# An encoder layer on one core: the FFN norm factor carried to the last norm, a running PSUM bank in the FFN input, and all pair weights of the FFN output prepared there

## The chip, the core and the metric

The kernel runs on one core of a Trainium2 chip. The core has five engines with queues of their own: TensorE (PE; its weight loads are listed apart as PEld), VectorE (DVE), ScalarE (ACT), GpSimd (POOL) and SyncE (SP). Each runs its own instructions in order and waits on semaphores for the others. All DMAs of this kernel are issued from SP's queue, in order. The metric is the device time of one launch in microseconds (us), the median of several launches.

## The reference

An encoder layer is applied to two sequences of 512 tokens (1024 tokens together, model width 1024), each with a memory of 256 rows: a norm, three branches (a state-space scan, a differential attention, a cross-attention on the memory), gates, an output projection, and then the part that the change touches:

```python
    x = x + merged @ p['w_out'][l]
    xn2 = _rmsnorm(x, p['norm_ffn'][l])
    gate, up = jnp.split(xn2 @ p['w_ffn_in'][l], 2, axis=-1)
    return x + (jax.nn.silu(gate) * up) @ p['w_ffn_out'][l]
    ...
    return _rmsnorm(x, p['norm_final'])
```

with `_rmsnorm(x, g) = x * rsqrt(mean(x*x) + 1e-6) * g`, and an FFN width of 2816.

## The kernel before

All is float32. Each product is made of three TensorE matmuls on rounded halves (`split`, L131: a ScalarE copy to the high half, a VectorE subtraction for the low half): high x high, high x low, low x high. Activations lie with features on the partitions, 128 at a time, and the 1024 tokens on the free side, the two sequences as two halves of 512 (`L`). The matmuls around the change have 512 columns.

**Seven products instead of eight.** The FFN's two matrix products take 2 x 2 blocks (two feature blocks, two halves of the tokens) and form them with seven products of sums and differences. The weights' names are A11, A12, A22 (plain blocks) and S1 to S4 (sums, made by POOL); the operands' sums stand in `ops` and `pairs`. The results are four quadrants: in the FFN input c11 and c12 are the gate of the two sequences, c21 and c22 the up part; in the FFN output they are two output tiles of 128 features by two sequences.

**FFN input** (L1134, 22 tiles, i = 0 to 21). A tile multiplies two 128-column weight blocks, one of w_fg and one of w_fu. `weights4` (L1002) loads both (`wf`, two buffers, L1006 and L1007), splits A11, A12 and A22, lets POOL form S1 to S4 (L1022 to L1025), and splits these. `products` (L1071) runs the seven products in the order A11, S2, A12, S3, S1, A22, S4, each into its own PSUM bank, 12 matmuls each. `quadrants` (L1104) copies the first bank by ScalarE (L1107) and forms the quadrants by six VectorE sums (`summed`, L1098, L1101), each of a bank and an SBUF tile. Then, per sequence: VectorE multiplies the gate by the norm's factor (`accs`, L1163), ScalarE takes a tanh (L1164), POOL multiplies up by the factor (L1165), VectorE multiplies twice (L1166, L1167) into `ac`, which goes to DRAM as aD. In tile 0 the factor is made out of the sums of squares: ones matmuls, a square root, a reciprocal, transposes and a copy (`rstd`, `factor`, L187 to L202).

**FFN output** (L1246). 12 visits cover four pairs of output tiles; within a visit a few pairs of FFN blocks are accumulated into seven banks (`VISITS`, 36 pieces in all, 21 matmuls each), then `quadrants` forms four results, which POOL adds to `y`. y was loaded from x1D, the residual that the output projection stored (L961). The weights of a piece are seven split blocks, `weights7` (L1213), loaded two pieces ahead.

**Pieces prepared early.** `prepare` (L459) is a generator that works on pieces ahead of time: load the raw blocks (two DMAs, L442), split three of them (`part(n_, 4, ...)`), form four sums on POOL (`raw_sums`, L451), split these (`part(n_, 0, ...)`), and store the halves to DRAM (`wD`). `half_piece` (L491) runs one step of it. `NPREP = (16, 28)`: pieces 0 to 15 are prepared with all seven blocks within the cross-attention's steps (L728), pieces 16 to 27 with the four sums alone within FFN input tiles 1 to 18 (L1170). For pieces 16 to 27 the three plain blocks, and for 28 to 35 all seven, are made on the spot in the FFN output.

**The end.** After the pairs come the last four FFN blocks as plain products, tile by tile of y, with sums of squares; `final` (L1313) makes the last norm's factor and stores the output.

**What sets the order.** A scheduler places the instructions of each engine by priorities and a model of their times, except where they are kept in written order (`PE.on`, L57) or held behind another instruction (`tc.issue_after`). TensorE is in written order through the attention stages and from the last FFN input tile on; in FFN input tiles 0 to 20 it was the scheduler's. Buffers of a pool are handed round; an instruction that writes one waits for the last reader of what was there.

Of the kernel before, what the change touches and what calls it, by code (L numbers as in the profile page):

```python
# [39 lines left out]
NPREP = (16, 28)  # L40
# [32 lines left out]
def encoder(ctx: ExitStack, tc: tile.TileContext, a, out):  # L73
# [109 lines left out]

    def new_acc():
        return rp.tile([P, L], F32, tag="acc", name="acc", bufs=2)
# [9 lines left out]
    def factor(ss, n, nt=4, bias=epsc):  # L195

        rs = rp.tile([P, 4], F32, tag="rs", name="rs", bufs=4)
        S.activation(out=rs[:, :nt], in_=ss[:, :nt], func=AF.Sqrt, scale=1.0 / n, bias=bias)
        V.reciprocal(rs[:, :nt], rs[:, :nt])
        bc = aux()  # L200
        for t in range(nt):
            PE.transpose(bc[:, t * P : (t + 1) * P], rs[:, t : t + 1].broadcast_to([P, P]), ident)  # L202
        return rs, bc
# [235 lines left out]
    pieces = [(m, p, 7 if i < NPREP[0] else 4 if i < NPREP[1] else 0) for i, (m, p) in enumerate(pieces)]  # L439
# [19 lines left out]
    def prepare(es_, todo_):  # L459
# [130 lines left out]
    prep = prepare(pes, pieces[: NPREP[0]])  # L590
    next(prep)


# [97 lines left out]
    for i in range(-AHEAD, len(steps) + 1):  # L691
# [36 lines left out]
        half_piece(last_e)  # L728
    while queue:
        fill(6)  # L730
    assert next(prep, None) is None
    pes.close()
# [327 lines left out]
    def product(ps, w, o, ks=range(4)):  # L1060
        wh, wl = w
        for k in ks:
            th, tl = ops[k]
            ws_ = slice(k * P, (k + 1) * P)
            PE.matmul(ps, wh[:, ws_], th[:, o], start=(k == 0), stop=False)
            PE.matmul(ps, wh[:, ws_], tl[:, o], start=False, stop=False)
            PE.matmul(ps, wl[:, ws_], th[:, o], start=False, stop=(k == 3))
# [48 lines left out]

    def act_pair(p, tag="ts", third=PO):
# [16 lines left out]
    for i in range(KFF):  # L1134
        w = nxt_w or all7(i)
        nxt_w = None
        if i == 1:
            prep = prepare(pes, pieces[NPREP[0] : NPREP[1]])
# [10 lines left out]
        ps = products(i, w)  # L1149
        p0 = next(ps)  # L1150
        if i == 0:
            for s in range(NS):
                _, bc = rstd(accs[s], DM)
                S.copy(accs[s], bc)
        gf0, gf1, up0, up1 = quadrants(ps, p0)
        ac = ap2.tile([P, NT], F32, tag="ac", name="ac")
        with ExitStack() as es_:
# [3 lines left out]
            for s, gf, up in ((0, gf0, up0), (1, gf1, up1)):  # L1161
# [3 lines left out]
                PO.tensor_tensor(out=up, in0=up, in1=accs[s], op=ALU.mult)  # L1165
                V.scalar_tensor_tensor(out=ac[:, cs], in0=ac[:, cs], scalar=1.0, in1=gf, op0=ALU.add, op1=ALU.mult)  # L1166
# [132 lines left out]
    def ones(ss, sq, n, start=False, stop=False):  # L1299

        for t in range(n // P):
            PE.matmul(ss[:, t : t + 1], sq[:, t * P : (t + 1) * P], onec[:, 0:1], start=(start and t == 0),
                      stop=(stop and t == n // P - 1))

    def column_sums(acc, n):
        ss = aux()
        ones(ss, acc, n, True, True)
# [25 lines left out]
    for c, n in ((0, L), (L, L // 2), (L + L // 2, L // 2)):  # L1333
        acc = new_acc()
        for m in range(KD):
            if c == 0:
                if m == 0:
                    kept.insert(0, weight(last_rows(m), nb * P))
                if m < KD - 1:
                    with yielding(last_s if m == 0 else last_7):  # L1340
# [14 lines left out]
            if m == KD - 3:  # L1355
                ss = aux()
                ones(ss, acc, n, start=True)
# [8 lines left out]
        end = final(ss if c + n == NT else column_sums(acc, n), c, n, ready, (2, 3) if c == L else ())  # L1366
# [425 lines left out]
```

## Time and profile before

| | us |
|---|---|
| median of 3 launches | 1603.34 (1603.12 to 1603.37) |
| span of the profiled launch | 1603.0 |
| cross-attention with the early pieces | about 386 to 530 |
| FFN input, tiles 1 to 20, one unbroken run of matmuls | 971.7 to 1351.7 |
| FFN output, pieces | about 1352 to 1545 |
| last four blocks, last norm | 1545 to 1603 |

The profile is one launch, taken by the hardware profiler. In a row, "x" and a number is a count; "ns" or a plain number after busy time is the mean of one; a duration of a matmul covers its whole way through the array, so that rows overlap, and the pace is read from start to start or from a count per stretch. "<-" names what ended an idle time. Lines (L...) are those of the kernel before. In the table of stretches each engine has its busy time and, after x, its instructions; then follow the clock granted to TensorE, the share of the DMA engines' time, and GB/s. In the list of waits the numbers are the sum in us, the count and the longest.

### The profile page before, as it was taken

How to read it: one execution, taken by the hardware profiler on the slowest of the kernel's cores; microseconds unless marked ns; L12 is line 12 of the kernel's file. 1: busy time of each engine (PE TensorE's matmuls, PEld its weight loads, DVE VectorE, ACT ScalarE, POOL GpSimd, SP SyncE). 2: the span in 40 equal slices, each digit the busy share in tenths (PEclk: the TensorE clock that was granted, in tenths of full speed). 3: DMA queues.
4: the chain of work that ended last, by engine and by line, in shares of the span. 5: the costliest groups of instructions: out<-in, count | busy, mean ns of one | idle time of the engine just before them, and what ended most of it. 6: DMA issues, size and time to landing. Idle time of an engine off the chain costs nothing.

```text
span 1603.0 us, 21625 instructions
## 1 busy us (share of the span) xinstructions
PE 1587.1 (99%) x7838; PEld 1314.8 (82%) x7838; DVE 1162.9 (73%) x1856; ACT 640.0 (40%) x1142; POOL 541.6 (34%) x449
## 2 busy tenths in 40 slices
PE   9999999999999999999999999999999999999997
PEld 7888788888898778778878878888888888788877
DVE  7976996076773766776465678888898778988654
ACT  6544323274652455574133443332333323233323
POOL 0010100001333220300343367676665553444653
PEclk9999999999999999999999999999999999999998
DMA  9554523576762111244454432333323223986222
GB/s 366 173 160 150 179 95 125 180 273 201 252 224 102 54 47 40 73 156 140 145 190 132 144 118 80 131 119 129 121 106 118 79 88 119 344 332 198 80 66 106
DMA packets 104891, 237.86 MB, mean 148 GB/s; under 512 B 13520, under 2 KB 45008, under 8 KB 104784
## 3 DMA queue, kind: packets, MB, share of 16 engines
q1 hardware_dynamic: 104784, 236.47, 43.1%
q8 instruction: 62, 1.02, 0.3%
q14 instruction: 45, 0.37, 0.1%
HBM read 165.16 MB, written 71.27 MB: 147 GB/s over the span
## 4 chain that ended last, share of the span: by engine, by line
PE 87%; issue 4%; DVE 3%; DMA 3%; POOL 2%; ACT 0%; SPq 0%; POOLq 0%; DVEq 0%; ACTq 0%
PE bkmm L66 75%; PE bksc L66 3%; PE bktr L66 2%; PE bkoo L66 2%; PE bktr L69 2%; DVE tl L135 1%; PE bktr L1626 1%; POOL mg L793 1%; PE bktr L1597 1%; DMA yt<-bD 1%; PE bktr L1686 0%; PE bktr L1687 0%; PE bktr L1685 0%; PE bktr L1565 0%; DMA acc<-in_w_fo 0%
## 5 line engine op out<-in xcount | busy, mean ns | idle before, releaser
L66 PE MATMUL bkmm<-xh,wh 128*128 128x512 f32 x640 | 255.4, 399 | 0.0
L66 PE MATMUL bkmm<-xh,wl 128*128 128x512 f32 x640 | 250.9, 392 | 0.0
L66 PE MATMUL bkmm<-xl,wh 128*128 128x512 f32 x640 | 250.5, 391 | 0.0
L66 PE MATMUL bkmm<-tl,wh 128*128 128x512 f32 (+1 forms) x621 | 241.2, 388 | 1.4 <-DVE tl L135 1.4
L66 PE MATMUL bkmm<-th,wl 128*128 128x512 f32 (+1 forms) x621 | 241.0, 389 | 0.9 <-DVE wl L135 0.9
L66 PE MATMUL bkmm<-th,wh 128*128 128x512 f32 (+1 forms) x621 | 241.1, 389 | 0.0
L134 ACT CAST wh<-wf 128x1024 fp32r<-128x1024 f32 (+1 forms) x134 | 117.9, 880 | 224.1 <-PE bkmm L66 179.8
L135 DVE TENSOR_TENSOR wl<-wf,wh 128x1024 fp32r<-128x1024 f32 (+1 forms) x134 | 145.1, 1083 | 50.2 <-ACT wh L134 45.7
L66 PEld LDWEIGHTS bkmm<-xh,wh 128*128 128x128 f32 x640 | 120.3, 188 | 30.3 <-issue 7.9
L66 PE MATMUL bkmm<-th,w 128*128 128x512 f32 x432 | 141.5, 392 | 2.7 <-DVE up L1101 1.0
L66 PEld LDWEIGHTS bkmm<-xh,wl 128*128 128x128 f32 x640 | 120.2, 188 | 26.7 <-issue 1.3
L66 PEld LDWEIGHTS bkmm<-xl,wh 128*128 128x128 f32 x640 | 120.4, 188 | 22.4 <-issue 0.4
L66 PEld LDWEIGHTS bkmm<-tl,wh 128*128 128x128 f32 x621 | 116.6, 188 | 25.9 <-DVE tl L135 2.1
L66 PEld LDWEIGHTS bkmm<-th,wl 128*128 128x128 f32 x621 | 116.5, 188 | 25.7 <-DVE wl L135 1.7
L66 PEld LDWEIGHTS bkmm<-th,wh 128*128 128x128 f32 x621 | 116.6, 188 | 23.9
L1165 POOL TENSOR_TENSOR up<-up,acc 128x512 f32<-128x512 f32 x44 | 83.6, 1920 | 87.8 <-DVE up L1101 87.8
L454 POOL TENSOR_TENSOR raw<-raw 128x128 f32<-128x128 f32 x28 | 15.2, 545 | 284.4 <-DVE nb L545 206.5
L66 PEld LDWEIGHTS bkmm<-th,w 128*128 128x128 f32 x432 | 80.9, 188 | 23.8 <-DVE up L1101 3.4
L793 POOL TENSOR_TENSOR mg<-mg,gl 128x1024 f32<-128x1024 f32 x16 | 43.5, 2720 | 139.0 <-DVE gl L789 139.0
L548 ACT ACTIVATE e<-bksc,nb 128x512 f32<-128x512 f32 (+1 forms) x96 | 58.8, 615 | 73.5 <-DVE nb L543 51.9
L66 PE MATMUL bkmm<-tl,w 128*128 128x512 f32 x216 | 84.2, 390 | 0.0
L66 PE MATMUL bkmm<-yh,wh 128*128 128x512 f32 x192 | 75.9, 397 | 0.8 <-ACT wh L134 0.4
(641 smaller groups left out, 3527.8 us busy)
## 6 DMA issues: line engine op xcount, KB each, us to landing
wf<-in_w_in SPq DMA_DIRECT2D x40, 512.0 KB, 3.9
wD<-hl SPq DMA_DIRECT2D x28, 512.0 KB, 2.9
w<-wD SPq DMA_DIRECT2D x28, 512.0 KB, 5.0
gD<-gt SPq DMA_DIRECT2D x24, 512.0 KB, 2.8
gl<-gD SPq DMA_DIRECT2D x24, 512.0 KB, 3.4
wf<-in_w_fg SPq DMA_DIRECT2D x22, 512.0 KB, 3.7
wf<-in_w_fu SPq DMA_DIRECT2D x22, 512.0 KB, 3.6
aD<-ac SPq DMA_DIRECT2D x22, 512.0 KB, 3.1
```

The lines of the kernel that those rows point to most:

```text
L66: return self.put(self.eng.matmul(*args, **kw))
L69: return self.put(self.eng.transpose(*args, **kw))
L134: h = S.copy(hi, src)
L135: l_ = V.tensor_tensor(out=lo, in0=src, in1=hi.bitcast(F32), op=ALU.subtract)
L454: PO.tensor_tensor(out=a22, in0=a21, in1=a22, op=ALU.add)
L548: last_x = S.activation(out=e, in_=sc, func=AF.Exp, bias=nb, scale=scale, accum_out=sm)
L793: PO.tensor_tensor(out=mg[m], in0=mg[m], in1=gt, op=ALU.add)
L1165: PO.tensor_tensor(out=up, in0=up, in1=accs[s], op=ALU.mult)
L1597: PE.matmul(kp[64 * hf : 64 * hf + 48, g * 144 : (g + 1) * 144], l_[:, 2 * hf + g, :], o_[:, 4 * g4 + 2 * hf + g, :], start=(l_ is lr48), ...
L1626: PE.matmul(ps[:, g * P : (g + 1) * P], w_[:, gg * P : (gg + 1) * P], u_[:, 8 * o + gg, :], start=True, stop=True)
```

## The change

Four things are changed.

1. **The factor is carried through.** The FFN's up part is no longer multiplied by the norm's factor, so the FFN's result is too large by 1/factor = `root` per token. The residual is multiplied by root too: eight times, x1D is loaded, multiplied by POOL with root (broadcast over the partitions: `rbc`, four transposes and a copy per sequence), and stored again. The last norm then works on root times the true sum; its epsilon is replaced by `eroot` = eps x 1024 x root^2 per token, which a small matmul puts ahead of the sums of squares (`least`), and its square root takes a bias of 0 (`zeroc`).
2. **A running bank.** In tiles 1 to 20 `running` takes the place of `products` and `quadrants`. A11, S2, S3 and A22 are accumulated, one after the other, into the same bank `pu`; ScalarE copies pu after A11, S2 and S3, and VectorE forms c11, u4, c22 and c12 with these copies: four sums. The fourth quadrant is pu itself, read by the last multiplication. The products run in the order A11, A12, S2, S1, S3, S4, A22.
3. **All 36 pieces are prepared beside it**, all with seven blocks, none in the cross-attention: `between` runs a step at three places of a tile and the old place runs a fourth, so two pieces per tile for tiles 1 to 18. The buffers of the split halves are one of each size (there were two of the larger). The FFN output only loads.
4. **Order and room.** TensorE is in written order from tile 1. `mbc`, used much earlier, moves to another pool.

```diff
-NPREP = (16, 28)
+NPREP = 36
...
-    pieces = [(m, p, 7 if i < NPREP[0] else 4 if i < NPREP[1] else 0) for i, (m, p) in enumerate(pieces)]
+    pieces = [(m, p, 7 if i < NPREP else 0) for i, (m, p) in enumerate(pieces)]
...
-            hl = pq.tile([P, k, 2, P], F32R, tag=f"hl{k}", name="hl", bufs=k // 2)
+            hl = pq.tile([P, k, 2, P], F32R, tag=f"hl{k}", name="hl", bufs=1)
...
-        mbc = cst.tile([P, L], F32, name="mbc")
+        mbc = new_acc()
...
-    prep = prepare(pes, pieces[: NPREP[0]])
-    next(prep)
...
-        half_piece(last_e)
...
+    def running(w, between):
+
+        def copied(tag):
+            t_ = ap2.tile([P, L], F32, tag=tag, name=tag)
+            S.copy(t_, pu)
+            return t_
+
+        of = dict(SEVEN)
+        pu, pv = bank(), bank()
+        product(pu, w["A11"], of["A11"])
+        product(pv, w["A12"], of["A12"])
+        c11 = summed("gf", pv, copied("p1"), 2)
+        between()
+        product(pu, w["S2"], of["S2"], more=True)
+        pw = bank()
+        product(pw, w["S1"], of["S1"])
+        u4 = summed("p1", pw, copied("u2"))
+        between()
+        product(pu, w["S3"], of["S3"], more=True)
+        px = bank()
+        product(px, w["S4"], of["S4"])
+        c22 = summed("up", pw, copied("u3"), 2)
+        c12 = summed("gf", px, u4, 2)
+        between()
+        product(pu, w["A22"], of["A22"], more=True)
+        return c11, c12, pu, c22
...
+        def between():
+            if 1 <= i < KFF - 3:
+                half_piece((last_sum,))
+
+        PE.on = i > 0
+        if i in (0, KFF - 1):
+            ps = products(i, w)
+            p0 = next(ps)
+            if i == 0:
+                for s in range(NS):
+                    rt = root[:, 4 * s : 4 * s + 4]
...
+                    S.activation(out=rt, in_=ss[:, :4], func=AF.Sqrt, scale=1.0 / DM, bias=epsc)
+                    rs = rp.tile([P, 4], F32, tag="rs", name="rs", bufs=4)
+                    V.reciprocal(rs, rt)
+                    S.copy(accs[s], spread(rs))
+                    V.scalar_tensor_tensor(out=eroot[:, 4 * s : 4 * s + 4], in0=rt, scalar=EPS * DM, in1=rt, op0=ALU.mult, op1=ALU.mult)
...
+                for s in range(NS):
+                    S.copy(rbc[:, s * L : (s + 1) * L], spread(root[:, 4 * s : 4 * s + 4]))
+            gf0, gf1, up0, up1 = quadrants(ps, p0)
+        else:
+            gf0, gf1, up0, up1 = running(w, between)
...
-                PO.tensor_tensor(out=up, in0=up, in1=accs[s], op=ALU.mult)
...
+        if 2 <= i < 2 + KD:
+            xs_ = rbp.tile([P, NT], F32, tag="xs", name="xs")
+            nc.sync.dma_start(xs_, x1D[i - 2])
+            PO.tensor_tensor(out=xs_, in0=xs_, in1=rbc, op=ALU.mult)
+            nc.sync.dma_start(x1D[i - 2], xs_)
...
+    def least(c, n):
         ss = aux()
-        ones(ss, acc, n, True, True)
+        PE.matmul(ss[:, : n // P], ident, eroot[:, c // P : (c + n) // P], start=True, stop=False)
+        return ss
...
-        _, bc = factor(ss, DM, n // P)
+        _, bc = factor(ss, DM, n // P, zeroc)
```

More of the change, by code (lines that the diff above doesn't have):

```diff
@@ L1058, in encoder, with product @@
     aD = [drp.tile([P, NT], F32, name=f"aD{i}") for i in range(KFF)]
-    def product(ps, w, o, ks=range(4)):
+    def product(ps, w, o, ks=range(4), more=False):
         wh, wl = w
+        mark = {"skip_group_check": True} if more else {}
         for k in ks:
@@ L1147, in encoder @@
             PE.on = True
[L1149 to L1155, printed above, removed]
+        def between():
[8 more added lines that the diff above has]
+                    rt = root[:, 4 * s : 4 * s + 4]
+                    ss = aux()
+                    for t in range(4):
+                        PE.matmul(ss[:, t : t + 1], accs[s][:, t * P : (t + 1) * P], onec[:, 0:1], start=(t == 0), stop=(t == 3))
+                    S.activation(out=rt, in_=ss[:, :4], func=AF.Sqrt, scale=1.0 / DM, bias=epsc)
[3 more added lines that the diff above has]
+                    V.scalar_tensor_tensor(out=eroot[:, 4 * s : 4 * s + 4], in0=rt, scalar=EPS * DM, in1=rt, op0=ALU.mult, op1=ALU.mult)
+                rbp = pes.enter_context(tc.tile_pool(name="rb", bufs=1, side="right", reuse_waits="tile"))
+                rbc = rbp.tile([P, NT], F32, tag="rbc", name="rbc")
+                for s in range(NS):
[3 more added lines that the diff above has]
+            gf0, gf1, up0, up1 = running(w, between)
         ac = ap2.tile([P, NT], F32, tag="ac", name="ac")
```

35 lines of the change are left out of this document (20 added, 15 removed).

## The prediction

> **What bounds the kernel now.** I read the page first, then the stretches of the span, then the chain of waits and TensorE's waits by stretch.
>
> ```profile
> span 1603.0 us, 21625 instructions
> PE 1587.1 (99%) x7838; PEld 1314.8 (82%) x7838; DVE 1162.9 (73%) x1856; ACT 640.0 (40%) x1142; POOL 541.6 (34%) x449
> ```
>
> TensorE is never idle for long, but a matmul row overlaps the next one, so 99% says little. The count of matmuls per stretch says more:
>
> ```profile
> core 0: us, PE busy (x) PEld busy (x) DVE busy (x) ACT busy (x) POOL busy (x), PEclk, DMA share, GB/s
> 386.00:530.00 144.00, 144.00 (x800) 123.20 (x799) 92.44 (x235) 69.08 (x167) 44.68 (x73) 1.00 0.53 187
> 985.00:1061.00 76.00, 76.00 (x336) 62.65 (x335) 68.21 (x75) 24.23 (x33) 49.28 (x37) 1.00 0.36 120
> 1061.00:1155.00 94.00, 94.00 (x416) 77.86 (x415) 83.17 (x91) 29.67 (x40) 64.74 (x51) 1.00 0.38 126
> ...
> 1366.00:1400.00 34.00, 32.51 (x141) 25.87 (x141) 32.71 (x40) 8.71 (x12) 16.75 (x11) 1.00 0.98 369
> 1400.00:1440.00 40.00, 39.64 (x175) 32.48 (x174) 35.86 (x42) 13.97 (x17) 17.74 (x12) 1.00 0.93 348
> 1440.00:1520.00 80.00, 79.89 (x351) 65.41 (x350) 60.53 (x78) 24.74 (x37) 39.85 (x42) 1.00 0.44 144
> 1520.00:1545.00 25.00, 23.63 (x99) 17.87 (x97) 15.91 (x22) 8.89 (x17) 15.58 (x20) 1.00 0.34 106
> ```
>
> ```profile
> 971.71 379.99 PE bkmm L66 x1675
> ```
>
> The last row is one unbroken piece of the chain: 1675 matmuls of 512 columns in 379.99 us, 0.2268 us each, at a granted clock of 1.00. That is the FFN input, tiles 1 to 20, and it has no stall at all: 336 in 76 us and 416 in 94 us give 0.226 too. The change keeps all matmuls there (7 products of 12 per tile, 84 x 0.2268 = 19.05 us a tile), so this stage can only stay or get longer. In the FFN output, time minus count x 0.2268 leaves 2.0, 0.3, 0.4 and 2.5 us in the four stretches from 1366 on. This is what is to be had. What ends the waits there:
>
> ```profile
> PE bkmm L66 <- DVE up L1101: 1.0, 2, 0.7
> PE bkmm L66 <- DVE wl L135: 0.9, 1, 0.9
> ...
> PE bkmm L66 <- DMA w<-wD: 0.6, 1, 0.6
> ...
> PE bkmm L66 <- ACT w L137: 0.3, 1, 0.3
> PE bkmm L66 <- DVE w L138: 0.3, 1, 0.3
> ```
>
> **The change part by part.** *Pieces out of the cross-attention.* 16 pieces leave 386 to 530. There PE shows 144.00 of 144 us busy and no wait on a piece, so I cost it at 0; what stands in the way is nothing but TensorE's own work.
>
> *FFN output.* The last 20 pieces lose their splits, the last 8 also their sums on POOL. The waits on w (L137, L138) and on wl (L135, the last matrix's split, queued behind six others) sum to 1.5 us; the whole loss of 1520 to 1545 is 2.5. The change takes away what those engines do there, so I take that 2.5 and 0.3 of the 0.4 before it: -2.8 us. Least -1.5 (the three waits alone), most -5.2 (all four stretches). In their place come loads of 896 KB per piece of 21 matmuls (4.76 us), 193 GB/s, where 1400 to 1440 already carried 348 GB/s with 0.3 us lost.
>
> *Tile 0 and the end.* Eight transposes of root are new on TensorE, and three 2- or 4-column matmuls. A group of four:
>
> ```profile
> 971.12 0.60 PE L69 MATMUL bktr<-ident,rs 128*128 128x128 f32 x4
> ```
>
> Two groups are 1.2 us. They stand among the products of tile 1 in the built program, so nothing hides them: +1.2 (0.9 to 2, if one waits).
>
> *FFN input, an ordinary tile.* VectorE loses two sums, POOL two products; two pieces a tile come in, each with four POOL sums, two ScalarE and two VectorE splits and two stores. The new thing is the order: TensorE, which from tile 1 on keeps the written order, so that nothing passes a late product, now waits for ScalarE's copy of the running bank three times a tile, with one product (12 x 0.2268 = 2.72 us) to cover it. In the built program ScalarE's queue reads: split of S1/S2, piece split (3 blocks), piece split (4 blocks), third copy. The 4-block split waits for POOL's raw sums, these for the S sums of the next tile, these for its w_fu load, and that for the buffer freed by the split of A22, which is now the last product. So from the end of one A22 to the start of the next runs a chain, against 72 x 0.2268 = 16.3 us of matmuls. Its links in the tile of before:
>
> ```profile
> 1173.38 0.62 ACT L134 CAST wh<-wf 128x512 fp32r<-128x512 f32 x1 [1.63 <-PE bkmm L66]
> 1174.17 1.18 DVE L135 TENSOR_TENSOR wl<-wf,wh 128x512 fp32r<-128x512 f32 x1
> 1175.38 0.33 SPq L1007 DMA_DIRECT2D wf<-in_w_fu  x1
> 1179.32 1.51 POOL L1022 TENSOR_TENSOR ws<-wf 128x512 f32<-128x512 f32 x1 [2.82 <-ACT ac L1164]
> 1180.80 1.74 POOL L1025 TENSOR_TENSOR ws<-wf 128x512 f32<-128x512 f32 x1
> 1182.50 1.74 POOL L1023 TENSOR_TENSOR ws<-ws,wf 128x512 f32<-128x512 f32 x1
> 1184.32 1.63 POOL L1024 TENSOR_TENSOR ws<-wf,ws 128x512 f32<-128x512 f32 x1
> ```
>
> ```profile
> 1161.03 0.62 ACT L137 ACTIVATE hl<-raw 128x512 fp32r<-128x512 f32 x1
> 1161.55 0.57 ACT L1107 COPY p<-bkmm 128x512 f32<-128x512 f32 x1
> ```
>
> ```profile
> L455 POOL TENSOR_TENSOR raw<-raw 128x128 f32<-128x128 f32 x16 | 9.1, 569 | 1.3
> ...
> L455 POOL TENSOR_TENSOR raw<-raw 128x128 f32<-128x128 f32 x5 | 4.0, 794 | 0.4
> ```
>
> 0.62 + 1.18 + 3.94 (issue to first sum) + 6.63 (1179.32 to 1185.95) + 4 x 0.57 + 0.62 + 0.57 = 15.8 us: 0.5 short of the cover. Below: POOL alone, and a 0.69 split,
>
> ```profile
> 927.66 1.30 POOL L1022 TENSOR_TENSOR ws<-wf 128x512 f32<-128x512 f32 x1 [0.97 <-DMA wf<-in_w_fu]
> ...
> 1161.51 1.78 DVE L1166 SCALAR_TENSOR_TENSOR ac<-ac,gf 128x512 f32<-128x512 f32 x1
> ...
> 1170.03 0.69 DVE L1166 SCALAR_TENSOR_TENSOR ac<-ac,gf 128x512 f32<-128x512 f32 x1 [0.28 <-ACT ac L1164]
> ```
>
> gives 15.8 - 1.4 - 0.5 = 13.9, no loss. Above: raw sums at 0.79 (+0.9), one VectorE operation held up by POOL (1.78 for 0.69, +1.1) and the product with the running bank ahead of the split (+0.7): 18.5, or 2.2 us a tile. I take 0.15 us a tile, an estimate near the middle's zero: 14 tiles, +2.1 (0 to 31).
>
> *FFN input, tiles 1 to 4.* There the built program also puts the eight x1D scalings, two a tile, on POOL, with one buffer. One goes round as POOL, store, load:
>
> ```profile
> L793 POOL TENSOR_TENSOR mg<-mg,gl 128x1024 f32<-128x1024 f32 x16 | 43.5, 2720 | 139.0 <-DVE gl L789 139.0
> ```
>
> ```profile
> gl<-gD SPq DMA_DIRECT2D x24, 512.0 KB, 3.4
> ...
> aD<-ac SPq DMA_DIRECT2D x22, 512.0 KB, 3.1
> ...
> y<-x1D SPq DMA_DIRECT2D x8, 512.0 KB, 6.3
> ```
>
> 2.72 + 3.1 + 3.4 + two issues of 0.33 = 9.9 us; the other half of the tile is POOL's: 2.72 + 6.63 + 4 x 0.57 = 11.6. Together 21.5 against 19.05, 2.5 us late a tile. SP's queue is in order: a scaling's store holds up a piece's store, the next scaling's load and the next weights' load behind it until POOL is done. The transfers fit: pieces 2 x 1.18 MB, weights 1.05, result 0.52 and scalings 2 x 1.05 are 6.0 MB in 19.05 us, 317 GB/s, under the 369 of 1366 to 1400, but two and a half times the 126 of now. The S sums of tiles 4, 5 and 6 follow: 7.5 us less what slack there was at the start. Bounds: 0 (POOL alone at 1.30, 1.4 less in the half that it sets, and a slack that takes the rest) and 25 (loads of 6.3 us as for y, 5.8 more a tile). I take +4, a little over half of 7.5, since tile 1 starts with weights in hand.
>
> The Trainium skill, page "SBUF — State Buffer", section "SBUF: two separate sides", says that a POOL operation and a VectorE operation with two SBUF inputs exclude each other for a whole instruction. The rows 1.78 and 0.69 agree. By that rule each scaling may also hold VectorE for all of its length; no row here shows such a pair, and the sum above counts nothing for it.
>
> Sum: -2.8 + 1.2 + 2.1 + 4 = +4.5 on the profiled 1603.0, so 1607.5; the median shown, 1603.34, lies 0.3 above the span: **1607.8 us**.
>
> **The rivals.** *A, clean input stage.* The copies are always in time and the scalings fit: -2.8 + 1.2 = 1601.7. For it: the chain is 0.5 short of the cover and ScalarE is idle two thirds of 985 to 1061. Against it: three new waits a tile with 2.72 us each.
>
> *B, faster.* As A, and all FFN output waits go, since VectorE and ScalarE are free at each visit's end: -5.2 + 1.2 = 1599.3. Against it: the two waits on up (L1101) are the visits' own sums, which stay.
>
> *C, VectorE becomes the bound.* A tile without pieces:
>
> ```profile
> 1268.00:1287.00 19.00, 19.00 (x86) 15.73 (x85) 14.59 (x18) 5.64 (x7) 10.27 (x7) 1.00 0.24 83
> ```
>
> ```profile
> L138 DVE SCALAR_TENSOR_TENSOR hl<-raw,hl 128x512 fp32r<-128x512 f32 x5 | 8.9, 1773 | 0.0
> ...
> L1101 DVE TENSOR_TENSOR u<-bkmm,p 128x512 f32<-128x512 f32 x5 | 3.4, 678 | 0.0
> ```
>
> 14.59 less two sums of 0.68, plus four piece splits a tile that POOL holds up to 1.77 each, is 20.3 us, 1.3 over 19.05; over the 18 tiles with pieces +23, so 1603.3 - 1.6 + 23 = 1625. For it: POOL works right beside these splits, and their five rows in the input stage are all held up. Against it: in 386 to 530 the same split ran beside POOL's raw sums in 0.69 (11.0 us for 16), and POOL no longer multiplies up:
>
> ```profile
> L138 DVE SCALAR_TENSOR_TENSOR hl<-raw,hl 128x512 fp32r<-128x512 f32 x16 | 11.0, 688 | 0.7 <-ACT hl L137 0.4
> ```
>
> This is also what the skill's lock rule would make of the stage if every split met a POOL operation.
>
> **How the numbers follow.** Forecast 0.44 (1603 to 1615 by its bounds where they are likely), A 0.25, B 0.20, C 0.11. The measurement tells 0.2% (3.2 us) from no change. Faster by more takes B and the lowest edge of A: 0.22. Within it lies the rest of A and the lowest part of the forecast: 0.28. Slower: 0.50. The range, 1599 to 1618, reaches from B's time over A to the forecast with most of the scalings' upper bound, and leaves out C and half of B's own side, some 0.2.
>
> **What would show it.** Right: gaps of 0.3 to 2 us between products in the FFN input, ahead of S2, S3 or A22, put down to the copies of the running bank (L1124), most of them in the first six tiles; the last eight pieces at 4.76 us each; two groups of transposes more in tile 1. A is right if the input stage still runs at 0.2268 us a matmul from tile 1 to 20; B if the stretches of the FFN output do too. C is right if VectorE is busy all of a tile and gaps go on to the last tile with pieces. The forecast is wrong at its root if the stalls of the input stage sum to under 2 us, or if they stand at the weights of A11 rather than at the running bank.

## The result and the profile after

| | before | after |
|---|---|---|
| median of 4 launches each, same chip, us | 1603.23 (1602.76 to 1603.37) | 1667.87 (1666.94 to 1670.37) |
| after over before | | 1.0407, 95% interval 1.0392 to 1.0422 |
| span of the profiled launch, us | 1603.0 | 1666.8 |

The change costs 4.1%, 64.6 us. The forecast was 1607.8 and its range ended at 1618. The page of after begins:

```profile
span 1666.8 us, 21678 instructions
PE 1622.5 (97%) x7852; PEld 1319.9 (79%) x7852; DVE 1095.0 (66%) x1799; ACT 660.6 (40%) x1184; POOL 502.5 (30%) x413
```

By their shares of the span VectorE, ScalarE and POOL are no fuller than before; the time is not in their sums. Three views show where it is. First, stretches (as in the prediction: span, busy time and count of each engine, granted clock, DMA share, GB/s). After:

```profile
60.00:360.00 300.00, 300.00 (x1564) 246.45 (x1563) 208.66 (x391) 112.26 (x208) 12.83 (x23) 1.00 0.47 156
...
970.00:1080.00 110.00, 98.09 (x401) 76.35 (x402) 90.21 (x94) 45.40 (x69) 72.37 (x57) 0.95 0.64 221
1242.60:1263.70 21.10, 19.80 (x85) 15.70 (x85) 13.89 (x19) 8.34 (x14) 12.58 (x12) 1.00 0.55 187
1366.00:1420.00 54.00, 51.08 (x212) 40.96 (x213) 38.01 (x49) 19.54 (x27) 17.73 (x13) 0.97 0.41 142
...
1500.00:1592.00 92.00, 92.00 (x401) 75.01 (x400) 46.62 (x62) 14.47 (x18) 34.11 (x26) 1.00 0.65 225
```

Before, the first of these stretches:

```profile
60.00:360.00 300.00, 300.00 (x1597) 251.54 (x1596) 211.79 (x398) 118.29 (x217) 15.48 (x23) 1.00 0.49 162
```

Up to 360 no changed instruction runs but one small memset at the start. TensorE is busy all of it in both, at a granted clock of 1.00, and yet does 1564 matmuls where it did 1597: it is 2% slower in code that nobody touched. Second, what TensorE waits for in after, from 960 to 1420 (total, times, longest; before has no wait at all from 975 to 1345):

```profile
PE bkmm L66 <- ACT u L1124: 27.5, 21, 2.7
PE bkmm L66 <- DVE ac L1215: 2.7, 1, 2.7
PE bkmm L66 <- DVE tl L135: 1.4, 2, 1.0
PE bkmm L66 <- ACT p L1124: 1.2, 1, 1.2
```

Third, the start of each FFN-input tile, worked out from the trace (the first matmul of every 84), less the one before it:

```
tile        0    1    2    3    4    5    6 to 18 (each)   19   20   start of 0   start of 21
before    23.5 19.5 19.3 19.0 19.0 19.0   19.0            19.0 19.0     942.4       1347.4
after     23.6 22.2 23.7 24.8 25.6 21.6   21.0 to 21.1    19.5 19.5     953.6       1408.2
```

So of the 63.7 us between the two spans, 11.1 have gone before the FFN input starts, 22.1 in tiles 1 to 5, 26.4 in tiles 6 to 18, 1.1 in tiles 0, 19 and 20, and 3.0 from tile 21 to the end.

### The profile page after: what moved, and what is told of

Its sections match the earlier page's. It is cut to its first block, busy times and chain, and to the rows that moved or that the text cites. A ratio compares the mean times of both kernels' runs of the same rounds, so it can differ in the third digit from the quotient of the medians.

```text
span 1666.8 us, 21678 instructions
## 1 busy us (share of the span) xinstructions
PE 1622.5 (97%) x7852; PEld 1319.9 (79%) x7852; DVE 1095.0 (66%) x1799; ACT 660.6 (40%) x1184; POOL 502.5 (30%) x413
## 5 line engine op out<-in xcount | busy, mean ns | idle before, releaser
L66 PE MATMUL bkmm<-th,wh 128*128 128x512 f32 (+1 forms) x621 | 249.0, 401 | 31.8 <-ACT u L1124 27.5
L66 PE MATMUL bkmm<-xh,wl 128*128 128x512 f32 x640 | 254.7, 398 | 0.0
L66 PE MATMUL bkmm<-xl,wh 128*128 128x512 f32 x640 | 253.9, 397 | 0.0
L66 PE MATMUL bkmm<-tl,wh 128*128 128x512 f32 (+1 forms) x621 | 247.3, 398 | 1.4 <-DVE tl L135 1.4
L66 PE MATMUL bkmm<-th,wl 128*128 128x512 f32 (+1 forms) x621 | 246.0, 397 | 0.0
L135 DVE TENSOR_TENSOR wl<-wf,wh 128x1024 fp32r<-128x1024 f32 (+1 forms) x134 | 148.8, 1110 | 64.4 <-ACT wh L134 59.0
L757 POOL TENSOR_TENSOR t<-t,rs 128x512 f32<-128x512 f32 x16 | 26.0, 1627 | 451.5 <-DVE t L756 416.9
L66 PEld LDWEIGHTS bkmm<-th,w 128*128 128x128 f32 x432 | 81.2, 188 | 19.6 <-DVE up L1104 0.9
L135 DVE TENSOR_TENSOR wl<-ws,wh 128x1024 fp32r<-128x1024 f32 x44 | 66.4, 1509 | 41.3 <-ACT wh L134 41.3
L137 ACT ACTIVATE hl<-raw 128x384 fp32r<-128x384 f32 (+1 forms) x72 | 40.5, 576 | 123.0 <-POOL raw L466 86.3
```

The source lines that it names most:

```text
L66: return self.put(self.eng.matmul(*args, **kw))
L135: l_ = V.tensor_tensor(out=lo, in0=src, in1=hi.bitcast(F32), op=ALU.subtract)
L137: h = S.activation(out=hi, in_=src, func=AF.Copy, scale=scale)
L757: PO.tensor_tensor(out=t2, in0=t2, in1=rope[1], op=ALU.mult)
```

## The experiments

All ratios are to the kernel before, run on the same chip. Most medians are of 4 launches; e6 and e12 have 2, e13 has 5, e15 has 12. The runs come from several chips, on which the kernel before has medians of 1603.2 to 1604.3, so differences between runs on different chips are good to about 1 us.

| run | in a few words | median us | ratio, 95% interval |
|---|---|---|---|
| e1_pad32 | after, 32 bytes of filler | 1665.68 | 1.0381 (1.0362 to 1.0399) |
| e2_before_off32 | before, all left-side tiles 32 bytes lower | 1623.53 | 1.0121 (1.0106 to 1.0136) |
| e3_no_xs | e1 without the x1D scalings | 1653.16 | 1.0306 (1.0291 to 1.0321) |
| e4_copy_first | e1, a half step moved | 1662.97 | 1.0366 (1.0349 to 1.0383) |
| e5_off512 | after, 416 bytes of filler | 1652.27 | 1.0298 (1.0281 to 1.0316) |
| e6_off256 | after, 160 bytes of filler | 1651.65 | 1.0296 (1.0276 to 1.0317) |
| e7_raw_first | e5, S sums behind raw sums | 1627.22 | 1.0147 (1.0132 to 1.0163) |
| e8_xs_spread | e7, scalings spread, on POOL | 1628.86 | 1.0154 (1.0139 to 1.0169) |
| e9_xs_dve | e8, scalings on DVE | 1619.20 | 1.0094 (1.0077 to 1.0111) |
| e10_edge | e9, ts behind tile 20's products | 1614.88 | 1.0066 (1.0051 to 1.0081) |
| e11_sixteen_early | e10, 16 pieces beside cross-attention | 1616.78 | 1.0077 (1.0062 to 1.0092) |
| e12_no_running | e5 without the running bank | 1615.41 | 1.0071 (1.0050 to 1.0091) |
| e13_no_running_xs_dve | e12, scalings as in e9 | 1612.46 | 1.0059 (1.0046 to 1.0072) |
| e14_no_running_xs_pool | e12, scalings as in e8 | 1621.48 | 1.0107 (1.0092 to 1.0123) |
| e15_best | e13, 16 pieces beside cross-attention | 1602.06 | 0.9989 (0.9980 to 0.9998) |
| e16_best_xs_pool | e15, scalings as in the change | 1610.14 | 1.0041 (1.0028 to 1.0054) |

### Addresses: e1, e2, e5, e6

The change takes 2048 bytes (`mbc`) out of the pool of constants, which lies lowest in SBUF, and puts three small tiles in. In the two built programs every tile of the left side, weights among them, stands 1952 bytes lower; those of the right side have not moved. The theory: TensorE's pace depends on these places. The edits:

```diff
+    V.memset(cst.tile([P, 8], F32, name="pad_k"), 0.0)      (e1; 104 columns in e5, 40 in e6)
     epsc = cst.tile([P, 1], F32, name="epsc")
```

```diff
-    V.memset(cst.tile([P, 8], F32, name="pad_l"), 0.0)      (e2, in the kernel before)
```

> The changed kernel with 32 bytes more in the pool of constants and nothing else, so that every tile of the left side of SBUF, which the change had moved by -1952 bytes to addresses that leave 32 over when divided by 64, starts at a multiple of 64 again. Theory A (places: the half-line offset slows TensorE's reading of those tiles): 512-column matmuls back to 0.2268 us each in all stages, the first FFN-input matmul at about 942 us instead of 953.6, FFN output pieces at 4.08 us for 18 matmuls instead of 4.15, and about 11 + (2.4% of some 620 us of matmuls behind it, 15) = 26 us less: 1642 us, with the gap of 1.5 us ahead of A22 in every tile still there. Theory B (the chip or the run, or another effect of the changed stages): first FFN-input matmul still at 953, 1668 us.

> The kernel before without its 32-byte filler ahead of the constant epsc, so that every left-side tile lies 32 bytes lower, off the multiple of 64, and nothing else differs. Theory A (places): first FFN-input matmul about 953 us instead of 942, matmuls at 0.232 to 0.234 us where they were at 0.2268, and 1603 + 11 + some 15 = about 1629 us. Theory B (the slower pace comes from the changed stages or the run): 1603 us within 1 us, the pace 0.2268 throughout.

e2 settles it in the kernel before: 20 us for 32 bytes. The unchanged stretch of e2:

```profile
60.00:360.00 300.00, 300.00 (x1567) 246.20 (x1567) 208.75 (x391) 112.91 (x209) 15.56 (x23) 1.00 0.48 156
```

1567 matmuls, as in after. But e1, back on multiples of 64, came to 1570 and gained almost nothing (2.2 us of the 26 expected), so 64 was the wrong number. Each matmul record was then paired with the addresses in the built program: that of its streamed operand less that of the weights loaded for the next matmul, modulo 256, against the time from its start to the next start (512-column matmuls whose starts lie 200 to 260 ns apart):

```
           rest 0          other rests (count, median ns)
before     5588, 227       128: 47, 232
after      2210, 227       96: 517, 232    160: 2796, 234   32: 23, 234   224: 24, 234
e1         2248, 227       128: 3308, 232
e2         2245, 227       32: 2824, 234   224: 523, 234    96: 24, 232   160: 23, 232
e5, e6     5519, 5531: 227 128: 47, 232 (each)
```

> The changed kernel with 416 bytes of filler in the pool of constants and nothing else: every left-side tile then keeps its distance to the right-side tiles modulo 512 bytes as in the kernel before (the shift is -1536 bytes), though not modulo 1024. Theory A (in the runs so far a 512-column matmul takes 0.227 us where the address of its streamed operand and the address of the weights that are loaded for the next matmul differ by a multiple of 512 bytes, and 0.232 to 0.235 us at every other difference seen): matmuls at 0.227 in all stages, the first FFN-input matmul at 942 instead of 953 us, FFN output 4 us shorter; in the steady FFN-input tiles nothing, since there the round through ACT's copy sets 21 us whatever the matmuls take: 1668 - 11 - 4 = about 1653 us. Theory B (only the old addresses, multiples of 1024, are fast): 1666 us.

> As the run with 416 bytes of filler, with 160 bytes: the shift is -1792 bytes, so the distance between left-side and right-side tiles is off by 256 modulo 512. If the period of the rule is 256 bytes, the pace is 0.227 us everywhere and the time as with 416 bytes (1653 us); if it is 512, the pace is 0.232 to 0.235 us where a right-side operand meets left-side weights, the first FFN-input matmul stands at 952 to 954 us, and the time is about 1666 us.

e5 came to the microsecond (1652.27 for 1653), partly by luck, since its steady tiles are at 20.8 to 21.0 us, which wasn't expected: the first FFN-input matmul stands at 943.3, and the unchanged stretch has 1597 matmuls again. e6 says that the period is 256 bytes, not 512:

```profile
60.00:360.00 300.00, 300.00 (x1594) 251.26 (x1593) 211.06 (x396) 116.64 (x216) 15.48 (x23) 1.00 0.49 160
```

The addresses cost 15.6 us in the changed kernel. Whether the matmul's own weights or the next ones count isn't told apart: the two rests differ in only 12 to 170 records of each of these runs. That the distance counts and not the place itself shows in e2, address by address against before: 1719 records have both operands moved by 32 bytes and keep a median of 227, and 3436 have one of the two moved and take 232 to 234. The rest of a single matmul isn't all of it: 518 records of after whose operands both stay where e5 has them have a median of 231. Where the three matmuls on either side are at rest 0 too, the median is 227 in before, after, e1, e2 and e5. The Trainium skill, page "SBUF — State Buffer", section "SBUF: two separate sides", allows no contention on the engine side but at the pair of ports that VectorE and POOL share. Here TensorE loses 5 to 7 ns in 227 by where its own two operands lie to each other; the measurement decides, and what happens inside isn't shown.

### The scalings and the order: e3, e4, e7, e8, e9

```diff
-        if 2 <= i < 2 + KD:                                  (e3: all five lines out)
-            xs_ = rbp.tile([P, NT], F32, tag="xs", name="xs")
...
```

```diff
         u4 = summed("p1", pw, copied("u2"))
-        between()
         product(pu, w["S3"], of["S3"], more=True)            (e4)
...
         c22 = summed("up", pw, copied("u3"), 2)
+        between()
         c12 = summed("gf", px, u4, 2)
```

> The first experiment's kernel (32 bytes of filler) without the eight scalings of x1D by the root: their loads, their POOL multiplications and their stores are left out, so the residual goes into the last norm unscaled. Theory A (the POOL-store-load round of the scalings, two to a tile, is what stops tiles 1 to 5 and through these stops lowers the granted clock): against the first experiment's kernel the stalls of tiles 1 to 5 go, the granted clock between 970 and 1080 us is 1.00 instead of 0.95, and 10 to 18 us go (488 instead of 401 matmuls in 110 us are worth 19 us, less what the slow pace explains). Theory B (the start of the preparation or the running bank alone stops these tiles): under 3 us.

> The first experiment's kernel with the second half step of a tile issued behind the third copy of the running bank instead of ahead of it, so that ACT copies before it splits a piece's four blocks. Theory A (the round A22's end, load of w_fu, S sums, raw sums, split of four blocks, copy, A22 sets the period of the steady tiles): the 1.5 us gap ahead of A22 goes in tiles 5 to 18, the tile takes 19.05 us, and 14 x 1.5 = about 20 us go against the first experiment's kernel. Theory B (the copy is only the last waiter of a chain that has no slack elsewhere, such as POOL's sums or the load of w_fu): the gap moves to S2 or S3 of the next tile and less than 5 us go.

e3 leaves the scalings out, so the residual goes into the last norm unscaled. It takes 12.5 us less than e1; from 970 to 1080 it does 450 matmuls at a granted clock of 1.00 (e1: 404 at 0.95), and tiles 2 to 5 take the 21 us of the steady ones. Theory A holds. e4, 2.7 us less than e1, told nothing of its theories: a step is held behind VectorE's sum only, ScalarE's queue is free of that, and in the steady tiles the split of four blocks still stands right ahead of the third copy. What the steady tile of after does is read from its rows (start, duration, engine and line; in brackets the idle time ahead and its releaser):

```profile
1242.14 1.48 DVE L135 TENSOR_TENSOR wl<-ws,wh 128x1024 fp32r<-128x1024 f32 x1
...
1242.79 0.60 ACT L134 CAST wh<-wf 128x512 fp32r<-128x512 f32 x1
...
1243.55 0.95 DVE L1214 SCALAR_TENSOR_TENSOR ac<-ac,gf 128x512 f32<-128x512 f32 x1
...
1245.02 0.88 DVE L135 TENSOR_TENSOR wl<-wf,wh 128x512 fp32r<-128x512 f32 x1
...
1245.93 0.33 SPq L1009 DMA_DIRECT2D wf<-in_w_fu  x1
...
1250.28 2.25 POOL L1024 TENSOR_TENSOR ws<-wf 128x512 f32<-128x512 f32 x1 [4.93 <-DMA wf<-in_w_fu]
...
1259.20 0.46 POOL L466 TENSOR_TENSOR raw<-raw 128x128 f32<-128x128 f32 x1
...
1259.69 0.63 ACT L137 ACTIVATE hl<-raw 128x512 fp32r<-128x512 f32 x1 [3.04 <-POOL raw L466]
1260.23 0.57 ACT L1124 COPY u<-bkmm 128x512 f32<-128x512 f32 x1
```

This is the chain that the prediction laid out, link by link: the split of A22, the buffer, the load of w_fu, the S sums, the raw sums, the split of four blocks, the copy, and then A22 at 1260.85. The row also shows a way out: POOL stands 4.93 us waiting for w_fu, with raw sums behind it that need no load. e7 puts them first:

```diff
-        with tc.issue_after(last_p.ins):                     (e7)
+        with tc.issue_after(last_p.ins), tc.issue_after((first_raw or last_p).ins):
             for _ in wg:
```

> The kernel with 416 bytes of filler, and on POOL the S sums of the next tile issued behind the raw sums of the tile's first piece, not ahead of them: POOL does these raw sums in the 5 us in which it waits for w_fu, and the four-block split ahead of the third copy finds them done. Theory A (the round A22's end, w_fu, S sums, raw sums, split, copy, A22 sets 21 us): the gap ahead of A22 goes in the steady tiles, the tile takes 84 x 0.227 = 19.05 us, and 14 x 1.95 = 27 us go against the kernel with the filler alone: about 1626 us. Theory B (POOL or ACT has no room for this work in 19 us whatever its order): the gap moves ahead of S2, S3 or A11 and under 8 us go.

25.1 us less than e5, steady tiles of 19.4 to 19.6: theory A, all but 0.4 us a tile. Then the scalings, spread (e8) and moved to DVE (e9):

```diff
+        if i in range(2, 2 + 2 * KD, 2):
+            with tc.issue_after(stored.ins):
+                xs_ = rbp.tile([P, NT], F32, tag="xs", name="xs")
+                nc.sync.dma_start(xs_, x1D[i // 2 - 1])
+        if i in range(3, 3 + 2 * KD, 2):
+            with tc.issue_after(last_raw.ins):
+                PO.tensor_tensor(out=xs_, in0=xs_, in1=rbc, op=ALU.mult)      (e9: V, behind last_sum)
+                nc.sync.dma_start(x1D[i // 2 - 1], xs_)
```

> The run before it (filler, raw sums first), with the eight scalings of x1D spread: one load in each second tile from 2 to 16, issued behind that tile's store of aD, its multiplication on POOL behind the raw sums of the next tile, so that POOL never waits for the load. Theory A (what stops tiles 1 to 5 is POOL held at its queue's head by the store-load round of a scaling): the stalls and the half-speed matmuls between 970 and 1080 us go as they did without the scalings, 12 us less than the run before it, about 1613 us. Theory B (the scaling's cost is POOL's time itself, wherever it lies): the stalls come back in the later tiles, under 4 us go.

> The kernel with the spread scalings, with each scaling's multiplication on DVE, behind the last sum of the odd tile, in place of POOL. In the run before it the tiles with a scaling took 20.7 us and those without 19.4 to 19.9, and in the former DVE's product of ac by up (128x512) took 2.89 us where it takes 0.68 otherwise, while POOL's multiplication of 2.84 us ran. Theory A (POOL's long multiplication holds DVE off, and DVE's late split of a piece starts the raw sums, the S sums and the third copy late): on DVE the scaling takes 1.2 to 1.3 us, the tiles with one come down to the others, and 8 x 1.0 to 1.3 = 8 to 10 us go, about 1619 us. Theory B (any 1024-column operation more in these tiles, on either engine, costs the 1.3 us): 1627 to 1629 us.

e8 is a miss: spreading gained nothing, and every tile in which a scaling runs, tiles 4 to 18 by twos, took 20.7 to 20.9. Its rows say why (two of POOL, then two of DVE):

```profile
1193.10 0.79 POOL L466 TENSOR_TENSOR raw<-raw 128x128 f32<-128x128 f32 x1
...
1194.38 2.84 POOL L1226 TENSOR_TENSOR xs<-xs,rbc 128x1024 f32<-128x1024 f32 x1
...
1193.49 0.67 DVE L1218 TENSOR_TENSOR ac<-ac,bkmm 128x512 f32<-128x512 f32 x1
...
1194.89 2.89 DVE L1218 TENSOR_TENSOR ac<-ac,up 128x512 f32<-128x512 f32 x1
```

The product with up, both operands in SBUF, ends 0.56 us after POOL's multiplication; the same line with one operand in PSUM takes 0.67 beside one of POOL's raw sums. By the lock rule of the Trainium skill, page "SBUF — State Buffer", section "SBUF: two separate sides", the one that starts first has the shared pair of ports for its whole instruction; these rows agree. What is lost is DVE's 2.2 us, and behind it the piece's split, the raw sums, the S sums and the copy. On DVE (e9) the scaling takes 1.2 us, and 9.7 us went, where 8 to 10 were expected.

### The edge, and fewer pieces: e10, e11

```diff
-            with tc.issue_after(last_s[1].ins):              (e10)
+            with tc.issue_after(last_s[1].ins), tc.issue_after(last_ac.ins):
                 acts = [act_pair(0, "tsa"), act_pair(1, "tsb", V)]
```

> The run before it, with the sums of the first two FFN-output pairs (ts) issued on DVE behind the last product of tile 20's halves in place of ahead of it. In the runs so far TensorE stands 2.97 us before tile 21's first matmuls, put down to DVE's product of ac by the running bank, and some of the next matmuls run at half speed. Theory A (the bank that the running sum leaves in PSUM is released only by that product, and the product stands behind the ts sums on DVE): the stop shrinks below 0.7 us and 2.5 to 4 us go against the run before it. Theory B (ts is then late for the first FFN-output pair): the stop moves ahead of the first pieces, under 1 us goes.

e10: 4.3 us, a little over the 2.5 to 4 expected; the stop of 2.97 us is gone and none has taken its place. It had stood in after too, in the wait on ac (L1215) above: tile 20's running sum stays in its bank until a product that stood behind five ts sums.

```diff
+    prep = prepare(pes, pieces[: NPREP[0]], 2)               (e11, ahead of cross-attention's steps)
...
+        half_piece(last_e)
...
-            prep = prepare(pes, pieces[:NPREP])
+            prep = prepare(pes, pieces[NPREP[0] : NPREP[1]])
```

> The run before it, with the first 16 pieces prepared beside cross-attention again, as in the kernel before, and the other 20 beside the FFN input, a little over one piece in a tile in place of two. Theory A (36 whole pieces are more than POOL, DVE and ACT can do beside 19 us of matmuls with the S sums, so some stall stays in every order): the tiles come to 19.05 us from tile 3 on, the start of the preparation in tiles 1 and 2 costs less than 2 us, and 6 to 10 us go against the run before it: 1604 to 1608 us, with the cross-attention stage no longer than before. Theory B (the order was all of it): within 2 us of the run before it.

e11 is a miss: 1.9 us more than e10. Its profiled launch has tile 0 at 26.7 us in place of 23.5 (below), and tiles 7, 8, 15 and 16 at 20.2 to 22.5, all waiting for the running bank's copies. Which order does that wasn't followed up.

### Without the running bank: e12 to e16

```diff
-            gf0, gf1, up0, up1 = running(w, between)         (e12)
+            ps = products(i, w)
+            gf0, gf1, up0, up1 = quadrants(ps, next(ps), between=between)
```

> The kernel with 416 bytes of filler alone (scalings on POOL, S sums where the change has them), with the seven products of a tile in the order and the separate banks of the kernel before, and their sums on DVE; all 36 pieces are still prepared beside them, three half steps between the products and one at the tile's end. Theory A (the third copy of the running bank, which stands behind the four-block split on ACT, is what carries POOL's lateness to TensorE): the 1.7 us gap of the steady tiles goes, a tile takes 19.05 to 19.5 us, 1652 - 14 x 1.7 = about 1628 us. Theory B (any form of the tile is stopped by the preparation of two pieces): the tile still takes over 20.5 us, 1645 us or more.

> The run without the running bank (separate banks, 416 bytes of filler, all 36 pieces prepared beside the FFN input), with the scalings of x1D spread over every second tile and multiplied on DVE, their loads one tile ahead. In that run tiles 3 to 6 took 22.5, 22.2, 19.9 and 25.0 us and all others from tile 2 on 19.0 to 19.1. Theory A (these 13.4 us are the scalings' alone): all tiles from 2 on take 19.05 us, and the time is 1615 - 13 = about 1602 us, down to 1600 if the FFN output keeps the 5 us that it gained there. Theory B (the first pieces' loads or the preparation itself stop these tiles): the stops stay in tiles 3 to 6, 1612 us or more.

> The same with the spread scalings multiplied on POOL, behind the raw sums of the tile. Theory A (without the running bank no copy stands behind the split of a piece, so DVE held off for some 2 us by POOL's 2.84 us multiplication costs TensorE nothing): within 2 us of the run with DVE. Theory B (POOL holding DVE off delays the sums that release TensorE's banks or the weights' splits): the tiles with a scaling take about 20 us and it is 6 to 10 us slower than with DVE.

e12, 36.9 us under e5, beats its own expectation: tiles 7 to 20 at 19.0 without any change of order, all stops behind tile 1 in tiles 3 to 6 (22.5, 22.2, 20.0, 25.0). e13 cleans tiles 2 to 7, but tiles 8 to 19 now take 19.3 to 20.9, and it gains only 3.0; e14 loses 6.1. The stretches of single tiles tell what has happened (third figure: DVE). e12:

```profile
1267.10:1286.10 19.00, 19.00 (x86) 15.73 (x84) 18.60 (x22) 7.25 (x12) 13.33 (x13) 1.00 0.64 213
```

e13:

```profile
1283.30:1302.90 19.60, 19.41 (x85) 15.70 (x85) 18.85 (x23) 7.83 (x12) 13.29 (x12) 1.00 0.71 238
```

e14:

```profile
1228.90:1250.20 21.30, 19.33 (x85) 15.59 (x84) 20.78 (x21) 6.64 (x11) 16.28 (x13) 1.00 0.57 195
```

With separate banks and two pieces a tile DVE is busy 18.60 of 19.00 us: it just fits, and the first scalings of e13, in tiles 4 and 6, still fit beside it. Tiles 8 to 19 are together 9.6 us over 12 x 19.05; the six scalings in them are 6 x 1.21 = 7.3 us of DVE. What TensorE waits for in e13 from 1110 to 1345 is DVE's split of the weights:

```profile
PE bkmm L66 <- DVE wl L136: 3.4, 8, 1.4
PE bkmm L66 <- ACT wh L135: 0.4, 1, 0.4
```

The running bank had eased just this (13.89 of 21.10 in after) and had put ScalarE's copy into a round instead. Two sums less a tile are only 1.4 of the 4.7 us between the two kernels; the same operations also take longer in e12, as a product and a piece split show (two rows of after, two of e12; the number behind the busy time is the mean in ns):

```profile
L1212 DVE TENSOR_TENSOR gf<-gf,acc 128x512 f32<-128x512 f32 x2 | 1.4, 682 | 0.0
L138 DVE SCALAR_TENSOR_TENSOR hl<-raw,hl 128x512 fp32r<-128x512 f32 x2 | 1.4, 686 | 2.1 <-ACT hl L137 2.1
L1217 DVE TENSOR_TENSOR gf<-gf,acc 128x512 f32<-128x512 f32 x2 | 2.5, 1236 | 0.0
L139 DVE SCALAR_TENSOR_TENSOR hl<-raw,hl 128x512 fp32r<-128x512 f32 x2 | 2.5, 1236 | 0.4 <-ACT hl L138 0.4
```

Which POOL operations they meet there wasn't followed up. The way left is fewer pieces in a tile:

> Separate banks, filler, the first 16 pieces prepared beside cross-attention as in the kernel before and the other 20 beside the FFN input (a little over one piece in a tile), the scalings of x1D spread over every second tile on DVE. Theory A (DVE's room in the tile decides: two pieces and the S and product sums leave 0.4 us of 19.0, one piece some 2.5): all tiles from 2 on take 19.05 us, tile 21 starts at about 1349 us, the FFN output keeps its 5 us, and the time is 1599 to 1601 us, 0.2% below the kernel before; a run in which the clock falls in tile 0 is 3 us longer. Theory B (some part of the excess is in none of running bank, addresses, scalings and density): 1605 us or more.

> The same, with the scalings as the change has them (POOL, tiles 1 to 8, each load behind the store of the one before). Theory A (with one piece in a tile DVE and POOL have room, but POOL still waits at its queue's head for the round of store and load): stops in the tiles with two scalings, fewer than the 13.4 us that they cost with two pieces in a tile, 4 to 10 us over the run with DVE. Theory B (with room they cost nothing): within 1.5 us of it.

e15 in the chain of waits (start, length, count), and the last pieces of the FFN output:

```profile
979.60 374.06 PE bkmm L66 x1650
```

```profile
1480.00:1543.00 63.00, 63.00 (x281) 52.22 (x280) 28.57 (x42) 11.12 (x17) 20.36 (x16) 1.00 0.60 202
```

1650 matmuls in 374.06 us, 0.2267 each: the input stage is one unbroken piece again. From the start of tile 21 to the last matmul of the pieces it is 192.4 us (1349.4 to 1541.7) against 196.1 before (1347.4 to 1543.5). e15 is the one version that beats the kernel before, by 0.1% (interval 0.02 to 0.2%; its 12 launches lie between 1600.3 and 1606.9, the median a microsecond above the expected 1599 to 1601): it keeps the factor carried through and the 36 prepared pieces, 16 of them beside the cross-attention again, and drops the running bank, the change's addresses and the early scalings on POOL. e16: scalings as in the change cost 8.1 us more, as expected.

## Why the prediction was wrong

**The sign was right, the size was not.** Forecast +4.5, measured +64.6.

- *The step that failed first: an ordinary FFN-input tile, "I take 0.15 us a tile".* The mechanism was right, with its place and its releaser: one gap a tile ahead of A22, put down to L1124. Its size was not. From the end of A22 (1242.55, 12 matmuls of 0.2325 from 1239.76) to the next start at 1260.85 are 18.3 us, against 15.8 summed and 18.5 as upper bound. By links: split of A22 to issue of w_fu 3.35 for 1.80, since DVE does a weight split of 1.48 us and two products before its half; issue to first sum 4.38 for 3.94; S and raw sums 9.41 for 8.91; split and copy 1.16 for 1.19. A chain that closes on itself half a microsecond short of its cover was priced near its best case, and the links were taken from a tile with a third of the pieces (12 in 18 tiles, not 36). The cost was 2.0 us a tile and 26.4 in tiles 6 to 18, inside the stated bounds (0 to 31) but outside the range, which was drawn from the value taken. The sign "most of them in the first six tiles" failed with it. e7 shows the cause: another order on POOL takes 25.1 us off.
- *A term that was missing: the addresses, 15.6 us (e5, e6).* The text counts instructions and queues; that `mbc` moved to another pool has no line in it. "I cost it at 0" for the cross-attention was right of the pieces: in e5 the first FFN-input matmul stands at 943.3, 0.9 later than before.
- *The scalings, +4 (0 to 25).* e3 shows 12.5. The half with the queue (POOL, store, load) was only a part: spread out, with loads a tile ahead, they cost as much (e8). The part set aside in the sentence on the Trainium skill's lock rule ("the sum above counts nothing for it") was what decides: the pair that no row showed then is the 2.89 us row of e8, and e9 gains 9.7 us by leaving POOL.
- *The edge of tile 21, 4.3 us (e10), was not seen:* the fourth quadrant stays in PSUM, and its reader stood behind the ts sums.
- *The clock.* No term was made for it. In tiles 3 and 4 of after, and again from 1416, matmuls behind a stop run at half speed (last section).
- *FFN output, -2.8 (-1.5 to -5.2):* right, 0.9 too small. In e15, where nothing else disturbs it, the way from tile 21 through the pieces is 3.7 us shorter; the last pieces run without a stall, as said. In after the slow addresses (18 matmuls in 4.22 us or 4.08, for 4.08) and the edge had eaten it.
- *Tile 0 and the end, +1.2:* right in place and size: in e15 tile 1 takes 20.4 us for 19.5, 0.9 more.
- *Rivals.* A and B are wrong for this kernel; B's -5.2 for the FFN output is further from 3.7 than the forecast's -2.8. C (VectorE the bound, 0.11) is wrong here: its sum was 20.3 us a tile, and DVE is busy 13.89 of 21.10, since the piece splits that it priced at 1.77 took up to 0.69 (the row of L138 above). VectorE does come to the bound in the kernel without the running bank, 18.60 of 19.00 in e12, and C had no such kernel in view.

By single edits from after down, on medians: addresses 15.6, POOL's order 25.1, scalings 8.0 (e7 to e9), edge 4.3. The 10.6 us that e10 still has over its own runs of before (1614.88 to 1604.33) are, in the profiled launches, 13.8 more in tiles 1 to 17 (22.5 in tile 1, up to 20.8 in the others), 1.2 more in what lies ahead and in the other tiles, and 5.1 less from tile 21 on. How these divide wasn't taken further; e12 to e15 take the other way around.

## What to carry to other kernels

When an edit adds or takes bytes in a pool that lies below others, look at where every later tile has moved to, modulo 256, against the tiles that meet it on TensorE; a changed pace in a stage that was not edited is the sign. When a wait closes a round (the end of a product releases the load that the next but one depends on), list all that stands ahead of each link in its queue and price the round by its upper bound if it comes within a microsecond of its cover. Do not count POOL work as free for VectorE: ask for each POOL instruction which VectorE instruction it will meet, and who waits for that one.

## What the runs showed of the hardware that was not expected

**Addresses set TensorE's pace:** 227 ns for 512 columns where streamed operand and next weights agree modulo 256 bytes, 232 to 234 ns at rests of 32, 96, 128, 160 and 224 (table above), at a granted clock of 1.00.

**A stop of 2 to 3 us can be followed by half the clock for some 3.4 us.** TensorE in tile 3 of after:

```profile
1041.20 0.40 PE L66 MATMUL bkmm<-th,wl 128*128 128x512 f32 x1
1043.49 0.61 PE L66 MATMUL bkmm<-th,wh 128*128 128x512 f32 x1 [1.90 <-ACT u L1124]
1043.90 0.63 PE L66 MATMUL bkmm<-tl,wh 128*128 128x512 f32 x1
...
1046.89 0.52 PE L66 MATMUL bkmm<-th,wl 128*128 128x512 f32 x1
1047.25 0.40 PE L66 MATMUL bkmm<-th,wh 128*128 128x512 f32 x1
```

```profile
1043.40:1047.00 3.60, 3.50 (x9) 2.72 (x10) 3.60 (x5) 0.99 (x2) 1.24 (x2) 0.55 0.30 116
```

2.29 us from start to start, then eight matmuls at 0.43 us, at a granted clock of 0.55 in that stretch: 1.6 us more on top of the stop. It is not certain: the stop at the edge, 3.1 to 3.2 us from start to start in tile 21, was followed by slow matmuls in seven of the nine kernels that have it (after, e4, e5 to e9) and by none in e1 and e3, nor were two stops of 2.7 us in e12. The steady tiles' stops of 1.7 us in after had no such end. Yet the two stops within tile 0, 0.8 to 1.1 and 1.2 to 1.4 us from start to start and about 2.2 us apart, which are in every version, were at times followed by the slow clock: tile 0 took 26.7 us in the profiled launches of e5, e7, e11 and e13, and 23.5 to 23.6 in all others. These 3.2 us may be some of the spread of the launches here, which wasn't tested. The Trainium skill, page "TensorE: Matmul & The Clock Gate", section "What's actually happening", has the clock at half after an idle window of some 3.4 us and at full again after a busy one of that length, windows running free of the program. The length of the slow spell agrees (3.4 us from the first slow start to the last, 1043.49 to 1046.89), and so does it that like stops end differently; the idle time that led to it was shorter here.
